# Weight splits of a decoder layer moved within the attention steps, blocks of normed rows rebuilt from their parts, and another split of the last norm

## The chip, the cores and the metric

The kernel runs on one core of one Trainium2 chip. The metric is the device time of one execution in microseconds (us). Inputs are float32, and the kernel keeps float32 accuracy by splitting each matmul operand into a high and a low part (type float32r) and adding three products: high by high, high by low, low by high.

## What is computed

One decoder layer on 512 rows of width 1024. The input is normed, and one projection gives the inputs of two branches: sparse attention (an indexer picks 128 of 512 keys for each query; 8 heads share a latent of rank 128) and a gated short convolution. Each branch is projected, multiplied by a sigmoid gate, and the sum goes through one output projection and a norm. A gated MLP with a convolution of width 3 and a per-layer embedding (PLE) with its own gate follow, and a last norm.

```python
h = layer_norm(x, ln_emb_g, ln_emb_b)
proj = h @ w_in[i]
...
o_lat = dsa_sparse_attention(q_lat, c_kv, q_idx, k_idx, w_idx)
att = jnp.einsum('bshr,hrd->bshd', o_lat, w_uv[i]).reshape(bsz, seq, ATT_WIDTH)
conv_y = cv_b * causal_dwconv(cv_c * cv_x, mix_conv_w[i], mix_conv_b[i])
merged = (jax.nn.sigmoid(g_att + b_gate[i, 0]) * (att @ w_br_att[i])
          + jax.nn.sigmoid(g_conv + b_gate[i, 1]) * (conv_y @ w_br_conv[i]))
h = layer_norm(DEEPNORM_ALPHA * h + merged @ w_o[i], ln1_g[i], ln1_b[i])
gu = causal_dwconv(h @ w_ffn_up[i], ffn_conv_w[i], ffn_conv_b[i])
g_ffn, u_ffn = jnp.split(gu, 2, axis=-1)
ffn = (jax.nn.silu(g_ffn) * u_ffn) @ w_ffn_down[i]
ple = jax.nn.sigmoid(h @ w_ple_gate[i] + b_ple_gate[i]) * (p[i] @ w_ple[i])
h = layer_norm(DEEPNORM_ALPHA * h + ffn + ple, ln2_g[i], ln2_b[i])
```

## The kernel before

The program is a list of steps, each of which is mostly one weight tile (128 x 1024 float32, a `Chunk`) and its 24 matmuls. `run` (L1356) goes through them in order: for step i it first calls `advance(i)`, then the small jobs hung on that step (`preps`), then the step itself. The instructions of each engine run in the order in which they are written down here, so a job's place in this list is its place in the queue of its engine.

`advance(i)` (L1338) does the weights. It splits the tiles that are due, mostly three steps before they are needed: `Chunk.split` (L53) has ScalarE copy the raw tile into the high part (L62), and `low` (L122, L123) subtracts that from the raw tile to give the low part, on VectorE (`lo="v"`) or GpSimd (`lo="p"`). As soon as a raw tile is used up, SyncE loads a later one; four raw tiles, four high and four low ones are in rotation.

From `at_first` on a list called `order` gives the steps: a convolution step (place 0), the four query projections (1 to 4), nine more convolution steps (5 to 13), then gates and branch projections from place 14 to 37. At eleven of them, places 12, 14, 16, 18, 20, 21, 22, 24, 26, 27 and 28 (`ATT_AT`), `with_att` (L786) puts a part of the attention ahead of the step's own matmuls. Such a part (`att_step`, L639) works on three blocks at once: latent output of the block two back (`att_c`: matmuls `ol`, evacuated by ScalarE and VectorE), transposes of the probabilities of the block one back (`att_b`: `pT`, matmuls of L606, which read `p`), and the logits of a new block (`att_a`: matmuls `lg`, their maximum on VectorE at L586 and L589, exponentials on ScalarE at L592, scaling of `p` by VectorE at L598). Tiles at places up to 28 have their low part made by GpSimd, later ones by VectorE. VectorE also works off the search for the top 128 keys (L535, L537) between the steps; it ends about place 13. GpSimd adds the taps of the convolution (L679), which VectorE then reads at L695.

DMAs on GpSimd's queue add up weights in DRAM (`weight_add`, L1056) that the MLP reads later: 28 of them, one at each place from 8 to 35. Copies that they need go out on SyncE's queue at places 0 to 13.

After the output projection (`wo_half1`, one step for each block of 128 rows) comes the first norm (`ln1`, L876): VectorE statistics, GpSimd's power (`rstd`, L155), VectorE's two passes L879 and L880. The block before is then transposed (`ln1_T`, `put_T`, L97): TensorE's transposes L105, an evacuation into high (ScalarE, L126) and low (VectorE, L127) parts, and a third copy of the same PSUM tile by ScalarE (L111) into `hblock`. During the steps of the PLE gate (`ple_gate`, `ple_gate1`, eight steps before the MLP) VectorE forms differences of these blocks (`row_sums`, L1065 and L1067) and splits them (`row_parts`), for the part of the MLP that works by blocks (`by_blocks`), which multiplies them.

The last norm (`last_norm`, L1279) of block 2 is shared: ScalarE and GpSimd do columns 0 to 447 (L1288 to L1290), VectorE the rest (L1295, L1299). Block 3 ends the kernel: its last sums (L1221), statistics, GpSimd's `rstd` and VectorE's four passes, then the stores.

Of the kernel before, what the change touches and what calls it, by code (L numbers as in the profile page):

```python
# [13 lines left out]
P = 128  # L14
# [51 lines left out]
class Kern:  # L66
# [27 lines left out]
        self.hTt = [self.main.tile([P, 4, 2, S], F32R, name=f"{name}{i}", tag="hT", bufs=2) for i in range(2)]  # L94
        self.hT = [self.hTt[c // 4][:, c % 4] for c in range(KC)]

    def put_T(self, b, h, keep=None):  # L97

        nc = self.nc
        tb = slice(b * P, (b + 1) * P)  # L100
        for g in range(2):
            t = self.ps("xT")
            for i in range(4):
                c = 4 * g + i
                nc.tensor.transpose(t[:, i * P:(i + 1) * P], h[:, c * P:(c + 1) * P], self.ident)  # L105
            t4 = t.rearrange("p (c t) -> p c t", c=4)
            self.evac_split(self.hTt[g][:, :, 0, tb], self.hTt[g][:, :, 1, tb], t4)
            if keep is not None:
                if b % 2 == 0:
                    keep[g, b // 2] = self.k4(f"hr{g}{b // 2}", F32, (P, 4, 256))  # L110
                nc.scalar.copy(keep[g, b // 2][:, :, b % 2 * P:b % 2 * P + P], t4)  # L111

    def k2(self, name, dt=F32, shape=(P, 512)):
        return self.main.tile(list(shape), dt, name=name, tag="k2", bufs=8)
# [337 lines left out]
    def plan(self):  # L452
        nc, a = self.nc, self.a
        self.steps = []
        self.chunks = []
        self.preps = {}
        self.nd = self.ns = 0

        def chunk(src, **kw):
            c = Chunk(self, src, **kw)  # L460
            self.chunks.append(c)
            return c
# [9 lines left out]
        def wa(i, **kw):  # L472
            return chunk(a["w_a"][i], **kw)
# [310 lines left out]


        def with_att(n, fn):  # L786
            def f():
                att_step(n)()
                fn()
            return f  # L790

# [12 lines left out]
        order += [("g", j, i) for j in (6, 7) for i in range(2)] + [("r", 3, 1), ("r", 3, 0)]  # L804
        for i, o in enumerate(order):
            if o[0] == "g":
                w = wa(20 + 2 * o[1] + o[2], lo="p" if i <= max(att_at) else "v")
                fn = gate(o[1], o[2], w)
            elif o[0] == "r":
                w = chunk(a["w_br"][2 * o[1] + o[2]], lo="p" if i <= max(att_at) else "v")  # L810
                fn = branch(o[1], o[2], w)
            elif o[0] == "q":
                w = wa(4 + o[1], lo="v" if o[1] == 1 else "p")
                fn = qatt(o[1], w)
            else:
# [14 lines left out]


        self.h1 = []
        self.hblock = {}

        def res_load():

# [46 lines left out]
        def ln1_T(b):  # L883
            if b == 0:
                self.new_hT("h1T")
            self.put_T(b, self.h1[b], self.hblock)

        def wo_half1(b, ws):
            def f():
# [161 lines left out]
        def weight_add(j, i):  # L1051
# [3 lines left out]
                        (s1[:, :512], s0[:, 512:]), (s1[:, 512:], u[:, :512]))[i]  # L1055
            return lambda: nc.gpsimd.dma_start(to, what, accum_op=OP.add, max_dma_last_dim=4096)  # L1056

        def row_sums(n):
# [80 lines left out]

        at_ff = len(self.steps)  # L1140
        for n in range(4):
            self.preps.setdefault(at_ff - 7 + n // 2, []).append(row_sums(n))
            self.preps.setdefault(at_ff - 4 + n, []).append(row_parts((0, 2, 1, 3)[n]))
        late_step, when = None, []
        for j in range(NF):
            if j in BY_BLOCKS:
                ws = [wa(36 + 2 * j)] + [chunk(t) for t in wsum[j]]
                for n, w in enumerate(ws):
                    step(by_blocks(j, n, w), [w])
                late_step = j  # L1150
                continue
            for which in (0, 1):
                when.append(len(self.steps))
                w = wa(36 + 2 * j + which)
                step(ffn(j, which, w), [w])
                if late_step is not None:
                    w = wa(37 + 2 * late_step, cols=(512, 1024))
                    step(by_blocks(late_step, 3, w), [w])
                    late_step = None
        self.preps.setdefault(len(self.steps), []).append(do_later)  # L1160
        for n, (j, i) in enumerate((j, i) for i in range(2) for j in BY_BLOCKS):
            self.preps.setdefault(at_first + n, []).append(weight_copy(j, i))
        for n, (j, i) in enumerate((j, i) for i in (0, 3, 1, 2) for j in BY_BLOCKS):
            self.preps.setdefault(at_first + 8 + n, []).append(weight_add(j, i))
        for n, (name, i) in enumerate(copies):
            self.preps.setdefault(at_first + self.SUM_AT + n, []).append(sum_copy(name, i))
            self.preps.setdefault(when[n], []).append(sum_add(name, i))
# [109 lines left out]
            return mv, self.rstd(mv[:, 1:2])  # L1277

        def last_norm(b):  # L1279
            by_pool = (0, 0, 448, 0)[b]  # L1280
            z, st = self.h1[b], self.st2[b]
            rows = self.out[b * P:(b + 1) * P, :]
            gb = [[t[q.start // 512][:, q.start % 512:][:, :q.stop - q.start] for t in (self.g2, self.b2)]
                  for q in (slice(0, by_pool), F1, slice(by_pool, 512))]
            if by_pool:
                mv, r, nmr = self.ln_aggr(st)
                q = slice(0, by_pool)
                nc.scalar.activation(z[:, q], z[:, q], AF.Identity, bias=nmr, scale=r)  # L1288
                nc.gpsimd.tensor_tensor(z[:, q], z[:, q], gb[0][0], op=OP.mult)
                nc.gpsimd.tensor_tensor(z[:, q], z[:, q], gb[0][1], op=OP.add)  # L1290
            else:
                mv, r = self.mv2.pop(b) if b in self.mv2 else mean_rstd(st)
            qs = list(zip([F1, slice(by_pool, 512)], gb[1:]))
            for q, (g, _) in qs:
                nc.vector.scalar_tensor_tensor(z[:, q], z[:, q], mv[:, 0:1], g, op0=OP.subtract, op1=OP.mult)  # L1295

# [58 lines left out]

    def run(self):  # L1356
        for i, fn in enumerate(self.steps):
            self.advance(i)
            for f in self.preps.get(i, ()):
                f()  # L1360
            fn()
# [99 lines left out]
```

## Time and profile before

| | us |
|---|---|
| median of 3 runs | 768.21 |
| lowest, highest | 768.02, 770.25 |
| the profiled execution | 769.37 |
| its span, first to last instruction | 767.3 |
| of it with TensorE busy | 749.9 |
| with VectorE, ScalarE, GpSimd busy | 557.5, 365.6, 247.1 |
| mean granted TensorE clock | 0.992 |

Engines in the rows: PE is TensorE (PEld its weight loads), DVE VectorE, ACT ScalarE, POOL GpSimd, SP SyncE. A row of the timeline gives start, duration, engine, line, operation, tiles written and read, the count of merged instructions, and in brackets the idle time before it and what ended it. TensorE's matmuls overlap, so their starts tell more than their durations: in steady work one of 512 columns starts every 0.227 us.

### The profile page before, as it was taken

The numbers are of one execution on the slowest core, as the hardware profiler recorded it, in microseconds if no ns is written. First come the engines' busy times: TensorE is split into PE (matmuls) and PEld (weight loads), VectorE is DVE, ScalarE is ACT, GpSimd is POOL, SyncE is SP. The second block draws the span as 40 slices with busy tenths as digits, with TensorE's granted clock in tenths as the row PEclk, the third lists the DMA queues.
The fourth block names the chain that finished last, engine by engine and source line by source line (L and its number), as shares of the span: only waits on it lengthen the run. The fifth ranks groups of instructions, "written<-read, shape, count | busy, mean of one in ns | idle before, by whom it ended". The sixth has DMA issues, their size and how long they took to land.

```text
span 767.3 us, 10309 instructions
## 1 busy us (share of the span) xinstructions
PE 749.9 (98%) x3831; PEld 635.5 (83%) x3831; DVE 557.5 (73%) x888; ACT 365.6 (48%) x561; POOL 247.1 (32%) x201
## 2 busy tenths in 40 slices
PE   7999999989999999999999999999999999999995
PEld 5998888878878888888788999998998888888885
DVE  5878999765655457958667777877777656788697
ACT  4556434466566425233335555555553433565540
POOL 4324666753415118956312311011112110100002
PEclk9999999999999999999999999999999999999998
DMA  8362576774323636996536756676668842656561
GB/s 322 103 236 94 167 218 191 207 192 110 99 66 95 140 130 253 299 339 212 220 110 234 190 179 184 178 203 195 189 192 213 199 136 70 205 180 233 187 210 56
DMA packets 41267, 138.84 MB, mean 181 GB/s; under 512 B 4945, under 2 KB 5073, under 8 KB 40833
## 3 DMA queue, kind: packets, MB, share of 16 engines
q1 hardware_dynamic: 31584, 112.21, 41.5%
q0 software_dynamic: 8624, 23.73, 16.5%
q10 hardware_dynamic: 1008, 2.25, 0.8%
q8 instruction: 30, 0.49, 0.2%
q14 instruction: 21, 0.16, 0.1%
HBM read 132.92 MB, written 45.09 MB: 232 GB/s over the span
## 4 chain that ended last, share of the span: by engine, by line
PE 74%; DVE 15%; POOL 3%; issue 3%; DMA 2%; ACT 2%; SPq 0%; DVEq 0%; POOLq 0%; ACTq 0%
PE ffb L1085 9%; PE ff L138 7%; PE ff L137 7%; PE ff L139 7%; PE dn L1215 4%; PE dn L1216 4%; PE dn L1214 4%; PE gt L137 3%; PE gt L138 3%; PE gt L139 3%; DVE tk L537 3%; DVE m L535 3%; DVE score L525 3%; POOL wl L123 2%; PE br L137 2%
## 5 line engine op out<-in xcount | busy, mean ns | idle before, releaser
L123 DVE TENSOR_TENSOR wl<-wr,wh 128x1024 fp32r<-128x1024 f32 x128 | 163.1, 1283 | 54.8 <-ACT wh L62 54.7
L62 ACT CAST wh<-wr 128x1024 fp32r<-128x1024 f32 (+1 forms) x163 | 164.2, 1011 | 80.9 <-PE dn L1216 35.0
L123 POOL TENSOR_TENSOR wl<-wr,wh 128x1024 fp32r<-128x1024 f32 x35 | 88.3, 2524 | 87.3 <-ACT wh L62 82.9
L137 PE MATMUL ff<-h1T,wh 128*128 128x512 f32 x240 | 93.5, 390 | 0.0
L138 PE MATMUL ff<-h1T,wh 128*128 128x512 f32 x240 | 93.5, 390 | 0.0
L139 PE MATMUL ff<-h1T,wl 128*128 128x512 f32 x240 | 93.4, 389 | 0.0
L665 DVE SCALAR_TENSOR_TENSOR ff<-ff,vec,ff 128x511 f32<-128x511 f32 x30 | 22.4, 747 | 47.6 <-ACT ff L664 47.6
L664 ACT ACTIVATE ff<-ff,vec 128x512 f32<-128x512 f32 x30 | 23.4, 779 | 65.5 <-PE ff L139 65.2
L139 PEld LDWEIGHTS ff<-h1T,wl 128*128 128x128 f32 x240 | 45.1, 188 | 9.4
L137 PEld LDWEIGHTS ff<-h1T,wh 128*128 128x128 f32 x240 | 45.1, 188 | 9.0
L138 PEld LDWEIGHTS ff<-h1T,wh 128*128 128x128 f32 x240 | 45.1, 188 | 8.9
L137 PE MATMUL gt<-hT,wh 128*128 128x512 f32 x128 | 51.1, 399 | 0.5 <-DVE ol L127 0.5
L138 PE MATMUL gt<-hT,wh 128*128 128x512 f32 x128 | 50.2, 393 | 0.0
L139 PE MATMUL gt<-hT,wl 128*128 128x512 f32 x128 | 50.1, 391 | 0.0
L155 POOL TENSOR_TENSOR rstd<-veps,neghalf 128x1 f32<-128x1 f32 x12 | 11.6, 963 | 107.9 <-DVE veps L153 81.0
L1016 POOL TENSOR_TENSOR T<-T,B 128x256 f32<-128x256 f32 x11 | 9.2, 835 | 99.0 <-DVE T L1014 99.0
L1020 POOL TENSOR_TENSOR T<-T,ff 128x256 f32<-128x256 f32 x11 | 8.1, 737 | 98.9 <-DVE T L1012 98.9
L1085 PE MATMUL ffb<-hsh,wl 128*128 128x256 f32 x112 | 31.7, 283 | 0.0
L1085 PE MATMUL ffb<-hsl,wh 128*128 128x256 f32 x112 | 31.7, 283 | 0.0
L1085 PE MATMUL ffb<-hsh,wh 128*128 128x256 f32 x112 | 31.7, 283 | 0.0
L137 PE MATMUL cv<-hT,wh 128*128 128x512 f32 x80 | 31.4, 392 | 0.0
L139 PE MATMUL cv<-hT,wl 128*128 128x512 f32 x80 | 31.1, 389 | 0.0
(318 smaller groups left out, 2002.2 us busy)
## 6 DMA issues: line engine op xcount, KB each, us to landing
wr<-in_w_a SPq DMA_DIRECT2D x73, 512.0 KB, 3.7
wr<-in_w_b SPq DMA_DIRECT2D x17, 512.0 KB, 4.6
wr<-in_w_dn SPq DMA_DIRECT2D x15, 512.0 KB, 3.3
ws<-in_w_a SPq DMA_DIRECT2D x28, 256.0 KB, 5.5
wr<-ws SPq DMA_DIRECT2D x14, 512.0 KB, 3.9
wr<-in_w_br SPq DMA_DIRECT2D x8, 512.0 KB, 3.3
ws<-in_w_a POOLq DMA_DIRECT2D x14, 256.0 KB, 5.6
ws<-ws POOLq DMA_DIRECT2D x14, 256.0 KB, 7.3
```

The lines of the kernel that those rows point to most:

```text
L62: nc.scalar.copy(hi, raw)
L123: (self.nc.vector if eng == "v" else self.nc.gpsimd).tensor_tensor(lo, raw, hi.bitcast(F32), op=OP.subtract)
L137: t.matmul(out, wh, xh, start=start, stop=False)
L138: t.matmul(out, wh, xl, start=False, stop=False)
L139: t.matmul(out, wl, xh, start=False, stop=stop)
L525: nc.vector.scalar_tensor_tensor(sc, rl, self.widx[b][:, h:h + 1], prev, op0=OP.mult, op1=OP.add)
L535: nc.vector.max(m8, cur)
L664: nc.scalar.activation(dst, src, AF.Identity, bias=v[:, bcol:bcol + 1], scale=v[:, wcol + 2 * tap:wcol + 2 * tap + 1])
L1085: nc.tensor.matmul(o, l[:, c], r, start=start and c + i == 0, stop=stop and c == 3 and i == 2, skip_group_check=True)
L1214: nc.tensor.matmul(o, ah, wh[:, i, c], start=first, stop=False, skip_group_check=bank == "X")
L1215: nc.tensor.matmul(o, ah, wl[:, i, c], start=False, stop=False, skip_group_check=bank == "X")
L1216: nc.tensor.matmul(o, al, wh[:, i, c], start=False, stop=last, skip_group_check=bank == "X")
```

## The change

Six edits:

1. At the eleven places with an attention part, `advance` moves from ahead of the step to between the attention part and the step's own matmuls. The jobs in `preps` then stand ahead of both.
2. Tiles of places 16 to 28 have their low part made by VectorE, not GpSimd: 13 tiles.
3. The 28 `weight_add` DMAs are put at places 8 to 28, four to every three places, instead of at 8 to 35, one to each.
4. `put_T` no longer makes the third copy. `row_block` has VectorE add the high and the low parts into the blocks, two at the second and two at the third step of the PLE gate; `row_sums` move two steps later.
5. The last norm of block 2: ScalarE and GpSimd take columns 0 to 511, VectorE 512 to 1023.
6. The loop that lays out the MLP's steps is written in another way, with the same order of steps and tiles for the blocks in use (1, 3, 5 to 13 by twos).

```diff
-    def put_T(self, b, h, keep=None):
+    def put_T(self, b, h):
...
-            self.evac_split(self.hTt[g][:, :, 0, tb], self.hTt[g][:, :, 1, tb], t4)
-            if keep is not None:
-                if b % 2 == 0:
-                    keep[g, b // 2] = self.k4(f"hr{g}{b // 2}", F32, (P, 4, 256))
-                nc.scalar.copy(keep[g, b // 2][:, :, b % 2 * P:b % 2 * P + P], t4)
+            self.evac_split(self.hTt[g][:, :, 0, tb], self.hTt[g][:, :, 1, tb],
+                            t.rearrange("p (c t) -> p c t", c=4))
...
+        self.own_advance = set()
...
         def with_att(n, fn):
+            i = len(self.steps)
+            self.own_advance.add(i)
+
             def f():
                 att_step(n)()
+                self.advance(i)
                 fn()
...
-                w = wa(20 + 2 * o[1] + o[2], lo="p" if i <= max(att_at) else "v")
+                w = wa(20 + 2 * o[1] + o[2], lo="p" if i < 16 else "v")
...
-                w = chunk(a["w_br"][2 * o[1] + o[2]], lo="p" if i <= max(att_at) else "v")
+                w = chunk(a["w_br"][2 * o[1] + o[2]], lo="p" if i < 16 else "v")
...
+        def row_block(g, h):
+
+            def f():
+                t = self.hblock[g, h] = self.k4(f"hb{g}{h}", F32, (P, 4, 256))
+                hi, lo = (self.hTt[g][:, :, i, 256 * h:256 * h + 256].bitcast(F32) for i in range(2))
+                nc.vector.tensor_tensor(t, hi, lo, op=OP.add)
+            return f
...
-            self.preps.setdefault(at_ff - 7 + n // 2, []).append(row_sums(n))
+            self.preps.setdefault(at_ff - 7 + n // 2, []).append(row_block(n // 2, n % 2))
+            self.preps.setdefault(at_ff - 5 + n // 2, []).append(row_sums(n))
...
-            self.preps.setdefault(at_first + 8 + n, []).append(weight_add(j, i))
+            self.preps.setdefault(at_first + 8 + 3 * n // 4, []).append(weight_add(j, i))
...
-            by_pool = (0, 0, 448, 0)[b]
+            by_pool = b == NB - 2
...
-                q = slice(0, by_pool)
-                nc.scalar.activation(z[:, q], z[:, q], AF.Identity, bias=nmr, scale=r)
-                nc.gpsimd.tensor_tensor(z[:, q], z[:, q], gb[0][0], op=OP.mult)
-                nc.gpsimd.tensor_tensor(z[:, q], z[:, q], gb[0][1], op=OP.add)
+                nc.scalar.activation(z[:, F0], z[:, F0], AF.Identity, bias=nmr, scale=r)
+                nc.gpsimd.tensor_tensor(z[:, F0], z[:, F0], gb[0][0], op=OP.mult)
+                nc.gpsimd.tensor_tensor(z[:, F0], z[:, F0], gb[0][1], op=OP.add)
...
-            qs = list(zip([F1, slice(by_pool, 512)], gb[1:]))
+            qs = [(F1, gb[1])] + ([] if by_pool else [(F0, gb[0])])
...
         for i, fn in enumerate(self.steps):
-            self.advance(i)
+            if i not in self.own_advance:
+                self.advance(i)
```

## Rows read from the trace of the kernel before

**Rows 1.** The page: busy time, share of the span and instructions of each engine.

```profile
PE 749.9 (98%) x3831; PEld 635.5 (83%) x3831; DVE 557.5 (73%) x888; ACT 365.6 (48%) x561; POOL 247.1 (32%) x201
```

**Rows 2.** Busy time by stretches of 20 us, with granted clock, DMA share, GB/s.

```profile
160.00:180.00 20.00, 17.97 (x85) 14.49 (x84) 11.83 (x24) 15.57 (x27) 9.35 (x6) 0.91 0.61 152
```

**Rows 3.** The waits of PE: for whom, us in total, times, longest.

```profile
PE pT L606 <- DVE p L598: 2.4, 2, 2.0
...
PE xT L105 <- DVE hr L880: 1.5, 1, 1.5
```

**Rows 4.** Timeline of PE about 160 to 168.

```profile
163.67 0.77 PE L606 MATMUL pT<-ident,p 128*128 128x128 f32 x5 [2.03 <-DVE p L598]
...
166.17 0.80 PE L137 MATMUL gt<-hT,wh 128*128 128x512 f32 x1
...
168.40 0.39 PE L139 MATMUL gt<-hT,wl 128*128 128x512 f32 x1
```

**Rows 5.** Timeline of DVE, 151 to 164.

```profile
151.22 0.69 DVE L695 TENSOR_TENSOR cvy<-cv,cvt 128x512 f32<-128x512 f32 x1 [0.98 <-POOL cvt L679]
...
156.12 1.86 DVE L589 TENSOR_SCALAR nmx<-mx 128x4 f32<-128x4 f32 x1
...
160.35 3.27 DVE L598 TENSOR_SCALAR p<-p,rs 128x256 f32<-128x256 f32 x4
```

**Rows 6.** Timeline of POOL, 155 to 158.

```profile
155.32 2.63 POOL L123 TENSOR_TENSOR wl<-wr,wh 128x1024 fp32r<-128x1024 f32 x1
```

**Rows 7.** Timeline of DVE, 169 to 174: L589 and L598 with no GpSimd work beside them.

```profile
169.45 0.17 DVE L589 TENSOR_SCALAR nmx<-mx 128x4 f32<-128x4 f32 x1
...
172.41 1.41 DVE L598 TENSOR_SCALAR p<-p,rs 128x384 f32<-128x384 f32 x4
```

**Rows 8.** Low parts: duration ns min/median/max; GpSimd's at 150 to 248, VectorE's of all.

```profile
L123 POOL TENSOR_TENSOR wl<-wr,wh x13: 2346/2397/2643, 151.1 to 245.1; 128x1024 fp32r<-128x1024 f32 x13
...
L123 DVE TENSOR_TENSOR wl<-wr,wh x128: 678/1219/3429, 24.5 to 748.9; 128x1024 fp32r<-128x1024 f32 x114, 128x512 fp32r<-128x512 f32 x14
```

**Rows 9.** Timeline of DVE, POOL and PE, 215 to 221.

```profile
215.09 3.30 DVE L598 TENSOR_SCALAR p<-p,rs 128x256 f32<-128x256 f32 x4
215.86 2.38 POOL L123 TENSOR_TENSOR wl<-wr,wh 128x1024 fp32r<-128x1024 f32 x1 [6.30 <-ACT wh L62]
...
218.45 0.77 PE L606 MATMUL pT<-ident,p 128*128 128x128 f32 x5 [0.38 <-DVE p L598]
...
220.93 0.47 PE L137 MATMUL gt<-hT,wh 128*128 128x512 f32 x1 [0.47 <-DVE ol L127]
```

**Rows 10.** Timeline of ACT, POOL, DVE and PE, 360 to 370.

```profile
360.22 0.59 ACT L111 COPY hr<-xT 128x512 f32<-128x512 f32 x1 [4.39 <-DVE h1T L127]
...
363.72 2.40 POOL L123 TENSOR_TENSOR wl<-wr,wh 128x1024 fp32r<-128x1024 f32 x1 [5.21 <-ACT wh L62]
363.76 3.44 DVE L879 SCALAR_TENSOR_TENSOR hr<-hr,mv,g 128x1024 f32<-128x1024 f32 x1
...
369.01 1.09 PE L105 MATMUL xT<-ident,hr 128*128 128x128 f32 x8 [1.54 <-DVE hr L880]
```

**Rows 11.** Timeline of DVE and POOL, 757 to 763.

```profile
757.71 1.87 DVE L1299 SCALAR_TENSOR_TENSOR hr<-hr,rstd,b 128x512 f32<-128x512 f32 x2
...
759.57 1.12 POOL L1290 TENSOR_TENSOR hr<-hr,b 128x448 f32<-128x448 f32 x1
...
760.77 1.41 DVE L1295 SCALAR_TENSOR_TENSOR hr<-hr,mv,g 128x512 f32<-128x512 f32 x2
```

**Rows 12.** Busy time of the two stretches in which VectorE gets more work; columns as in rows 2.

```profile
150.00:248.00 98.00, 94.87 (x474) 77.22 (x473) 56.75 (x135) 61.04 (x119) 43.13 (x28) 0.98 0.42 109
...
380.00:420.00 40.00, 40.00 (x182) 33.23 (x181) 25.84 (x28) 17.74 (x25) 5.76 (x5) 1.00 0.45 166
```

**Rows 13.** The page's groups of instructions: mean ns of ScalarE's high parts.

```profile
L62 ACT CAST wh<-wr 128x1024 fp32r<-128x1024 f32 (+1 forms) x163 | 164.2, 1011 | 80.9 <-PE dn L1216 35.0
```

**Rows 14.** The page's DMA issues: KB each, us from issue to landing.

```profile
wr<-in_w_a SPq DMA_DIRECT2D x73, 512.0 KB, 3.7
```

More of the change, by code (lines that the diff above doesn't have):

```diff
@@ L105, in put_T @@
                 nc.tensor.transpose(t[:, i * P:(i + 1) * P], h[:, c * P:(c + 1) * P], self.ident)
-            t4 = t.rearrange("p (c t) -> p c t", c=4)
-            self.evac_split(self.hTt[g][:, :, 0, tb], self.hTt[g][:, :, 1, tb], t4)
-            if keep is not None:
-                if b % 2 == 0:
-                    keep[g, b // 2] = self.k4(f"hr{g}{b // 2}", F32, (P, 4, 256))
-                nc.scalar.copy(keep[g, b // 2][:, :, b % 2 * P:b % 2 * P + P], t4)
+            self.evac_split(self.hTt[g][:, :, 0, tb], self.hTt[g][:, :, 1, tb],
+                            t.rearrange("p (c t) -> p c t", c=4))
     def k2(self, name, dt=F32, shape=(P, 512)):
@@ L832, in plan @@
         self.h1 = []
-        self.hblock = {}
         def res_load():
@@ L885, in ln1_T @@
                 self.new_hT("h1T")
-            self.put_T(b, self.h1[b], self.hblock)
+            self.put_T(b, self.h1[b])
         def wo_half1(b, ws):
@@ L1056, in weight_add @@
             return lambda: nc.gpsimd.dma_start(to, what, accum_op=OP.add, max_dma_last_dim=4096)
+        self.hblock = {}
+        def row_block(g, h):
[4 more added lines that the diff above has]
+            return f
         def row_sums(n):
@@ L1141, in plan, with last_block @@
         for n in range(4):
-            self.preps.setdefault(at_ff - 7 + n // 2, []).append(row_sums(n))
+            self.preps.setdefault(at_ff - 7 + n // 2, []).append(row_block(n // 2, n % 2))
+            self.preps.setdefault(at_ff - 5 + n // 2, []).append(row_sums(n))
             self.preps.setdefault(at_ff - 4 + n, []).append(row_parts((0, 2, 1, 3)[n]))
-        late_step, when = None, []
+        when, left = [], []
+        def last_block():
+            for j in left:
+                w = wa(37 + 2 * j, cols=(512, 1024))
+                step(by_blocks(j, 3, w), [w])
+            left.clear()
         for j in range(NF):
             if j in BY_BLOCKS:
-                ws = [wa(36 + 2 * j)] + [chunk(t) for t in wsum[j]]
-                for n, w in enumerate(ws):
+                for n in range(3):
+                    w = chunk(wsum[j][n - 1]) if n else wa(36 + 2 * j)
                     step(by_blocks(j, n, w), [w])
-                late_step = j
+                    if n == 0:
+                        last_block()
+                left.append(j)
                 continue
@@ L1155, in plan @@
                 step(ffn(j, which, w), [w])
[L1156 to L1159, printed above, removed]
+                last_block()
         self.preps.setdefault(len(self.steps), []).append(do_later)
@@ L1279, in last_norm @@
         def last_norm(b):
-            by_pool = (0, 0, 448, 0)[b]
+            by_pool = b == NB - 2
             z, st = self.h1[b], self.st2[b]
             rows = self.out[b * P:(b + 1) * P, :]
-            gb = [[t[q.start // 512][:, q.start % 512:][:, :q.stop - q.start] for t in (self.g2, self.b2)]
-                  for q in (slice(0, by_pool), F1, slice(by_pool, 512))]
+            gb = [[t[h] for t in (self.g2, self.b2)] for h in range(2)]
             if by_pool:
                 mv, r, nmr = self.ln_aggr(st)
-                q = slice(0, by_pool)
-                nc.scalar.activation(z[:, q], z[:, q], AF.Identity, bias=nmr, scale=r)
-                nc.gpsimd.tensor_tensor(z[:, q], z[:, q], gb[0][0], op=OP.mult)
-                nc.gpsimd.tensor_tensor(z[:, q], z[:, q], gb[0][1], op=OP.add)
+                nc.scalar.activation(z[:, F0], z[:, F0], AF.Identity, bias=nmr, scale=r)
+                nc.gpsimd.tensor_tensor(z[:, F0], z[:, F0], gb[0][0], op=OP.mult)
+                nc.gpsimd.tensor_tensor(z[:, F0], z[:, F0], gb[0][1], op=OP.add)
             else:
                 mv, r = self.mv2.pop(b) if b in self.mv2 else mean_rstd(st)
-            qs = list(zip([F1, slice(by_pool, 512)], gb[1:]))
+            qs = [(F1, gb[1])] + ([] if by_pool else [(F0, gb[0])])
             for q, (g, _) in qs:
```

## The prediction

> **What bounds the kernel now.** I read the page's busy times first: TensorE is busy nearly all of the span, so a faster helper engine gains nothing by itself [rows 1]. The question is only where TensorE waits, and whether the change reaches that place. The list of its waits answers this: after the start-up two matter, transposes of attention probabilities that wait for VectorE's scaling (2.4 us in two places) and transposes of the first norm's result that wait for VectorE's second pass (1.5 us) [rows 3]. Then the windows, for waits that the idle time does not show: the stretch 160 to 180 alone has a granted clock of 0.91 [rows 2]. The two levels are 1.2 and 2.4 GHz, so 0.09 x 20 / 0.5 = 3.6 us of it ran at the lower one. The timeline puts this behind the idle 2.03 us: between the gate's matmul at 166.17 and the one at 168.40 five starts take 2.23 us, where five steady ones take 5 x 0.227 = 1.14, so 1.09 us more is lost [rows 4]. All that the change can win lies in these few microseconds and in the tail behind the last matmul.
>
> **Edits 1 and 2, first place (160 to 168).** The chain that ends in the stall goes: convolution product L695, ScalarE's split of the next tile, ScalarE's and VectorE's copies of transposes, maximum, its negative (L589), exponentials, scaling (L598), transposes. Two VectorE operations in it are far too long: L589 on four columns takes 1.86 us, and the scaling of four pieces of 256 columns 3.27 us [rows 5]. Beside the first runs GpSimd's low part, 155.32 to 157.95, and L589 ends 0.03 us after it [rows 6]; another lies under the scaling. Undisturbed, L589 takes 0.17, and four pieces of 384 columns take 1.41 [rows 7], so four of 256 take at most that. VectorE thus stands still while GpSimd works, and 13 of GpSimd's low parts, 2.40 us each, go [rows 8]. They return on VectorE at 1.22 us each, 13 x 1.22 = 15.9 us.
> The new end of the chain: 160.35 + 3.27 = 163.62 before. Off: about 1.7 at L589 (1.86 less 0.17), 3.27 - 1.41 = 1.86 at the scaling, 1.01 for ScalarE's high part, which now stands behind the exponentials [rows 13]. On: the low part of place 16, which VectorE must do ahead of L695, where it is idle only because it waits for GpSimd's taps [rows 5]: 1.22. That is 160.3. The waiting transposes could have gone at 163.67 - 2.03 = 161.6 [rows 4], so 1.3 us are to spare and the wait of 2.03 goes; with no such idle I take the slow matmuls to go too: 2.03 + 1.09 = 3.1 us. The bounds: 1.0 (the first rival) and 3.1.
>
> **Second place (217 to 221).** The same picture, smaller: scaling 3.30 us with a GpSimd low part inside it, transposes 0.38 us late, and behind them the gate 0.47 us late, because VectorE's evacuations come after that scaling [rows 9]. With 1.41 at most in place of 3.30 the evacuations can start 1.9 us earlier, less the 1.22 of the low part now put between: still 0.7 earlier. I count both waits: 0.85 us, with 0.4 as the lower bound. What is late next there is the eight PSUM banks filling up, which leaves a few tenths of waits that I do not count as won.
>
> **What the moved step costs elsewhere.** A split comes later by its attention part, but its tile is needed three steps on, at least 3 x 24 x 0.227 = 16.3 us; if that cover went, TensorE would wait at the gate for the difference. Queued behind the moved splits: on ScalarE the next sigmoid, on VectorE the gate's products and the next attention part's evacuations, on SyncE the load of a later raw tile, which takes 3.7 us [rows 14] and has four steps. Past VectorE's queue: 56.75 busy of 98 us, 72.6 with the 15.9 [rows 12]. I put these at 0, up to +1.
>
> **Edit 3.** The same DMAs, issued up to seven places earlier. GpSimd has 43.13 busy us in the stretch [rows 12], of which 13 x 2.40 = 31.2 go; what is left is 12 us with 13 issues and two convolution operations in it, under 0.9 each. Their copies on SyncE's queue go out at places 0 to 13, ahead of each sum; the sums are read in the MLP, beyond 420 us. Cost 0; without the cover an issue ahead of the taps, 0.9.
>
> **Edit 4, first norm.** The stall at 369.01 comes from one GpSimd low part: it starts at 363.72, VectorE's pass L879 starts at 363.76 and takes 3.44 instead of about 1.3, and `rstd`, which L880 needs, stands behind it in GpSimd's own queue [rows 10]. That low part is so late because its high part stands on ScalarE behind the third copies (L111), the first of which waits 4.39 us for VectorE [rows 10]. Without them ScalarE does both evacuations of that block at once and the high part some 5 us sooner, GpSimd's low part follows the `rstd` of block 1, and block 2's norm meets it no more. The wait of 1.54 us goes; lower bound 0, if it meets the next pass instead.
> VectorE gains four additions, like a low part two float32 inputs of 1024 columns, so 4 x 1.22 = 4.9 us, in a stretch with 25.84 busy of 40 [rows 12]: 30.7 of 40. Its weight splits there run more than a step ahead of TensorE; the price if that cover went is what VectorE lags beyond it, so 0 to +1. I take 0.
>
> **Edit 5, tail.** GpSimd's last addition for block 2, 1.12 us for 448 columns, ends at 760.69, and block 3's pass L1295 starts 0.08 us behind it [rows 11]. 64 columns more are 1.12 x 64 / 448 = 0.16 on each of GpSimd's two operations and about 0.1 on ScalarE's, so GpSimd ends 0.4 later and holds VectorE so much longer. VectorE's two small pieces of 64 columns go, one of which waits inside the 1.87 us of L1299 [rows 11]; that brings the last sums some 0.3 sooner, in vain if L1295 is held. Cost +0.35, between -0.3 and +0.6. Edit 6 leaves the order of the work as it is: 0.
>
> **Sum.** -3.1 - 0.85 - 1.54 + 0.35 = -5.1 us. Against the profiled execution, 769.37, that is 764.2; this one lies 1.16 above the median of 768.21, so the median should be 763.1. With every bound at its good end -5.8, 762.4.
>
> **Rivals.**
> *VectorE's own split takes the lock's place at 161.* GpSimd still makes the low part of place 15, now between the attention part and the convolution of place 12, ahead of the taps. If that delays the taps by a whole low part, 2.4 [rows 8], the 1.3 to spare become 1.1 of idle and the clock may fall again, 1.09: of 3.1 about 1.0 is won. Sum -3.0, median 765.2. For it: L695 waits for the taps already [rows 5]. Against it: ScalarE's tap products are late too, and cover most of that low part.
> The Trainium skill, page SBUF — State Buffer, section Who interferes with whom, says that a VectorE instruction with two SBUF inputs and a GpSimd instruction that reads SBUF exclude each other, whoever starts first blocking the other for its whole length. By this rule the new splits on VectorE are themselves such instructions, and the tap adds and the split of place 16 can block one another, which speaks for this rival; L879 under GpSimd's low part [rows 10] agrees with it.
> *The first norm keeps its stall*: block 2's norm meets GpSimd at another moment. Sum -3.6, median 764.6. Against: `rstd` of block 2 then stands ahead of nothing but its own chain.
> *It does not do what it says.* The stalls at 161 and 369 re-form with other releasers, 0.5 won in all: 767.7.
> *Slower: the splits stand in front of the evacuations.* VectorE takes its queue in order. If a low part, waiting for ScalarE's high part, stands ahead of the latent output's evacuation, TensorE fills its eight banks and waits, as at 218 and 220.9, 0.85 us [rows 9], in each of the six attention parts that have transposes and no such stall now: +5.1, with the first two stalls kept, -1.54 and +0.35: +3.9, median 772.1. It decides from the point where a split ends later than the evacuation's input is ready by more than the few tenths that free banks give. For it: VectorE's 15.9 us more. Against: ScalarE's high parts come before the sigmoids, and the scaling gets shorter by more than a split lasts.
>
> **How the numbers follow.** The measurement of this kernel can tell about 0.3%, 2.3 us, from no change. Forecast 0.58, the first rival 0.16, the norm's 0.08, no effect 0.10, slower 0.08. Faster, below 765.9: 0.58 + 0.08 + three quarters of the first rival, 0.12, so 0.78; same 0.04 + 0.10 = 0.14; slower 0.08. The range leaves out the slow rival and some of no effect above, and goes 1.8 below the forecast for the few tenths at the banks and a lighter tail: 761.3 to 767.3.
>
> **What would show it.** Right: GpSimd without low parts from 150 to 250, scaling of 256 columns under 1.5 us, no PE row waiting for L598 near 161, granted clock 1.00 there, transposes of block 2 in the first norm without a wait, the last GpSimd addition ending later against the last matmul. Wrong: a wait of TensorE near 161 for VectorE or for a bank of equal size, a fall of the clock at another place, gates waiting for a low part, or the norm's passes again at 3 us.

## The result and the profile after

The changed kernel takes 762.97 us (median of 5 runs, 762.01 to 765.05). The kernel before, timed on the same chip beside it, takes 770.06 (5 runs, 768.02 to 771.99). The ratio is 0.9921 [0.9902, 0.9941]: faster, by 0.8%. 763.1 was forecast, within 761.3 to 767.3. The profiled execution of after took 764.64, with a span of 762.8 and a mean granted clock of 0.994.

Lines of the kernel after lie 3 to 4 lower in most places: L119 is the low part (L122, L123 before), L595 the scaling of `p` (L598), L603 the transposes of `p` (L606), L142 the logits (L146), L123 VectorE's evacuations (L127), L692 the convolution's product (L695). L879, L880 and L105 keep their numbers.

From the page of after: busy times, which answer [rows 1], and the chain of work that ended last, by engine.

```profile
PE 748.9 (98%) x3831; PEld 635.7 (83%) x3831; DVE 562.0 (74%) x903; ACT 361.7 (47%) x553; POOL 218.1 (29%) x188
...
PE 95%; DVE 3%; DMA 1%; ACT 0%; issue 0%; SPq 0%; DVEq 0%; ACTq 0%
```

GpSimd has lost 29 us; VectorE has gained 4.5, far less than the work put on it, since its long operations beside GpSimd went (the scalings together take 8.8 us less). TensorE is as busy as before. The head of the list of PE's waits, answering [rows 3]:

```profile
PE ckv L312 <- DVE hT L281: 2.2, 1, 2.2
PE warm L295 <- POOL ident masks.py:199: 1.4, 1, 1.4
PE ckv L308 <- ACT hT L277: 1.2, 2, 0.8
...
```

Both waits of [rows 3] are gone: no row of the whole list names the scaling or the norm's second pass. A new one of 2.2 us stands in the start-up, where the change moves no job (more of it in the part on the start-up). Windows of after, columns as in [rows 2]:

```profile
24.00:30.00 6.00, 6.00 (x39) 6.00 (x39) 4.21 (x8) 2.01 (x4) 2.59 (x4) 0.76 0.47 66
...
160.00:180.00 20.00, 20.00 (x106) 16.50 (x106) 13.35 (x30) 17.27 (x33) 8.69 (x11) 1.00 1.09 214
```

TensorE is busy for all of 160 to 180, at a granted clock of 1.00 where it was 0.91; what the mean clock of 0.994 still lacks lies in the start-up (0.76 in 24 to 30) and behind the last matmuls (0.66 in 755 to 762). The timeline of POOL, DVE and PE about the first place, answering [rows 4], [rows 5] and [rows 6] (this execution runs 2.62 us later than before's up to there, because of the start-up):

```profile
148.75 2.40 POOL L119 TENSOR_TENSOR wl<-wr,wh 128x1024 fp32r<-128x1024 f32 x1 [4.43 <-ACT wh L62]
151.12 2.64 POOL L676 TENSOR_TENSOR cvt<-cvt,tap 128x511 f32<-128x511 f32 x2
...
152.73 2.11 DVE L119 TENSOR_TENSOR wl<-wr,wh 128x1024 fp32r<-128x1024 f32 x1
154.76 0.68 DVE L692 TENSOR_TENSOR cvy<-cv,cvt 128x512 f32<-128x512 f32 x1
...
157.42 4.17 POOL L1056 DMA_DIRECT2D ws<-in_w_a  x5
...
158.72 0.28 DVE L586 TENSOR_SCALAR nmx<-mx 128x4 f32<-128x4 f32 x1
...
161.37 1.14 DVE L595 TENSOR_SCALAR p<-p,rs 128x256 f32<-128x256 f32 x4
...
163.78 1.03 PE L603 MATMUL pT<-ident,p 128*128 128x128 f32 x8
164.74 1.34 PE L142 MATMUL lg<-kT,qa 64*128 64x384 f32 x12
166.01 0.50 PE L133 MATMUL gt<-hT,wh 128*128 128x512 f32 x1
```

The negative maximum takes 0.28 us instead of 1.86, the scaling 1.14 instead of 3.27, and it ends at 162.51, 1.27 us ahead of the first of the eight transposes that read it. GpSimd's last low part up to 250 us is the one at 148.75. Beside the negative maximum it issues DMAs now (157.42), and they do not hold VectorE as the low part did. The second place (DVE, PE; [rows 9]) and the first norm (ACT, POOL, DVE, PE; [rows 10]) of after:

```profile
213.98 1.14 DVE L595 TENSOR_SCALAR p<-p,rs 128x256 f32<-128x256 f32 x4
215.04 1.22 DVE L119 TENSOR_TENSOR wl<-wr,wh 128x1024 fp32r<-128x1024 f32 x1
...
217.44 1.32 PE L142 MATMUL lg<-kT,qa 64*128 64x384 f32 x12
```

```profile
354.06 1.07 ACT L62 CAST wh<-wr 128x1024 fp32r<-128x1024 f32 x1
...
356.33 3.38 POOL L119 TENSOR_TENSOR wl<-wr,wh 128x1024 fp32r<-128x1024 f32 x1
...
360.86 1.27 DVE L879 SCALAR_TENSOR_TENSOR hr<-hr,mv,g 128x1024 f32<-128x1024 f32 x1
362.58 1.31 DVE L880 SCALAR_TENSOR_TENSOR hr<-hr,rstd,b 128x1024 f32<-128x1024 f32 x1 [0.44 <-POOL rstd L151]
...
365.17 1.03 PE L105 MATMUL xT<-ident,hr 128*128 128x128 f32 x8
```

ScalarE's high part is made at 354.06 instead of 362.59, GpSimd's low part is over 1.15 us before the norm of block 2 begins, and the transposes have no wait.

To see where the time went, I took the start of every matmul in after less the start of the same one before. The difference changes in few places, and these are the terms of the sum:

| place | forecast | after | changed kernel, second profile |
|---|---|---|---|
| start-up, to 25 us | 0 | +2.6 | 0.0 |
| 161 to 178 | -3.1 | -3.74 | -3.74 |
| 217 to 226 | -0.85 | -1.04 | -1.05 |
| 366 to 376, first norm | -1.54 | -1.77 | -1.77 |
| last matmul to VectorE's last pass | +0.35 | +0.07 | +0.47 |

The second profile is that of an execution of the changed kernel (762.4 us) whose start-up runs as before's does. Elsewhere the difference moves by less than 0.1 at a step.

### The profile page after: what moved, and what is told of

Read it like the earlier page. It is cut to its first block, busy times and chain, and to the rows that moved or that the text cites. A ratio compares the mean times of both kernels' runs of the same rounds, so it can differ in the third digit from the quotient of the medians.

```text
span 762.8 us, 10310 instructions
## 1 busy us (share of the span) xinstructions
PE 748.9 (98%) x3831; PEld 635.7 (83%) x3831; DVE 562.0 (74%) x903; ACT 361.7 (47%) x553; POOL 218.1 (29%) x188
## 4 chain that ended last, share of the span: by engine, by line
PE 95%; DVE 3%; DMA 1%; ACT 0%; issue 0%; SPq 0%; DVEq 0%; ACTq 0%
PE ffb L1095 9%; PE ff L133 7%; PE ff L135 7%; PE ff L134 7%; PE dn L1232 5%; PE dn L1233 5%; PE dn L1231 5%; PE gt L133 4%; PE gt L134 4%; PE gt L135 4%; PE cv L133 2%; PE cv L135 2%; PE cv L134 2%; PE br L133 2%; PE wo L754 2%; PE pg L753 2%
## 5 line engine op out<-in xcount | busy, mean ns | idle before, releaser
L119 DVE TENSOR_TENSOR wl<-wr,wh 128x1024 fp32r<-128x1024 f32 x141 | 177.5, 1269 | 45.3 <-ACT wh L62 45.3
L119 POOL TENSOR_TENSOR wl<-wr,wh 128x1024 fp32r<-128x1024 f32 x22 | 56.8, 2583 | 34.9 <-ACT wh L62 24.8
L744 POOL TENSOR_TENSOR mT<-sig,mT 128x512 fp32r<-128x512 f32 x8 | 13.1, 1664 | 85.4 <-ACT mT L743 85.4
```

What stands on the lines that cost most here:

```text
L119: (self.nc.vector if eng == "v" else self.nc.gpsimd).tensor_tensor(lo, raw, hi.bitcast(F32), op=OP.subtract)
```

## Experiments

My theory was that of the prediction: VectorE stands still beside GpSimd's low parts, and the late scaling costs the first two places, the late norm the third. The rivals: that only the order of ScalarE's and VectorE's queues counts (edit 1 alone), that the number of low parts on GpSimd counts (edit 2 alone), and that splits on VectorE stand in front of evacuations.

### Edit 2 alone: low parts on VectorE, still ahead of the attention part

```diff
-                w = wa(20 + 2 * o[1] + o[2], lo="p" if i <= max(att_at) else "v")
+                w = wa(20 + 2 * o[1] + o[2], lo="p" if i < 16 else "v")
-                w = chunk(a["w_br"][2 * o[1] + o[2]], lo="p" if i <= max(att_at) else "v")
+                w = chunk(a["w_br"][2 * o[1] + o[2]], lo="p" if i < 16 else "v")
```

> The kernel before with edit 2 alone: low parts of places 16 to 28 by VectorE, the advance where it was. Theory (GpSimd's low parts block VectorE, and the order matters as well): L589 near 161 falls from 1.86 to under 0.4 us and the scaling of 256 columns from 3.27 to 1.1 to 1.4, but the split of place 17 now stands ahead of the attention part in VectorE's queue, 1.22 us, and ScalarE's high part, 1.0, is still ahead of its copies: the transposes near 161 still wait, 0.3 to 1.2 us, with or without a fall of the clock. The second place (217 to 221) gains 0.8 to 1.0. From 25 us on 2 to 3.5 us are won. Rival (the engine is all that counts): the wait near 161 is gone, 3.7 us won there, as in the changed kernel. Rival (the order is all that counts): the wait stays at 1.5 us or more.

Measured: 767.02 us (766.42 to 770.66), ratio 0.9978 [0.9957, 0.9999]. The matmuls win 3.21 us at the first place, and no wait near 161 is listed any more. Both edits together win 3.74 there, so a part is left to edit 1, but as slower matmuls and not as the wait that I had expected: the scaling ends at 161.48, when the transposes, from 161.02, have begun, and from their start to the gate's there are 2.78 us, where after has 2.23. The second place wins 1.05. But 2.29 us are given back between, 1.84 of them at 181. Timeline of this kernel, ACT, DVE and PE:

```profile
160.34 1.14 DVE L598 TENSOR_SCALAR p<-p,rs 128x256 f32<-128x256 f32 x4
...
177.37 1.05 ACT L62 CAST wh<-wr 128x1024 fp32r<-128x1024 f32 x1
...
178.45 1.23 DVE L123 TENSOR_TENSOR wl<-wr,wh 128x1024 fp32r<-128x1024 f32 x1 [1.51 <-ACT wh L62]
179.59 0.42 DVE L127 TENSOR_TENSOR ol<-ol,ol 128x256 fp32r<-128x256 f32 x1
...
181.02 0.47 PE L137 MATMUL br<-cvT,wh 128*128 128x512 f32 x1 [1.79 <-DVE ol L127]
```

VectorE waits 1.51 us for ScalarE's high part, then makes the low part, and only then evacuates `ol`, for which TensorE waits 1.79. This is the mechanism of the prediction's slower rival, at one of the attention parts instead of six.

### Edit 1 alone: advance between the attention part and the step

```diff
+            i = len(self.steps)
+            self.own_advance.add(i)
+
             def f():
                 att_step(n)()
+                self.advance(i)
                 fn()
...
         for i, fn in enumerate(self.steps):
-            self.advance(i)
+            if i not in self.own_advance:
+                self.advance(i)
```

> The kernel before with edit 1 alone: advance between attention part and gate, the low parts still by GpSimd. Theory: ScalarE's high part and so GpSimd's low part come behind the exponentials; L589 is free (0.2 to 0.3 us), and the scaling starts before GpSimd's low part does, at most its last piece is caught. The wait near 161 falls to 0 to 0.5 us, the slow matmuls behind it go: 2.5 to 3.7 us won there, 0.3 to 1.0 at the second place. Rival (the engine is all that counts): scaling still over 2.5 us and the wait near 161 still over 1.5 us.

Measured: 768.4 us (768.24 to 771.08), ratio 0.9992 [0.9974, 1.001]. The first place wins all of its 3.74 us here too, though its scaling still takes 3.3 us: it starts early enough. The second place wins nothing, 1.96 are given back at 195 to 199, and 0.75 at 251. DVE, POOL and PE of this kernel:

```profile
187.28 5.98 DVE L599 TENSOR_SCALAR p<-p,rs 128x512 f32<-128x512 f32 x4
...
188.05 4.92 POOL L123 TENSOR_TENSOR wl<-wr,wh 128x1024 fp32r<-128x1024 f32 x2 [10.63 <-ACT wh L62]
...
193.31 1.64 PE L607 MATMUL pT<-ident,p 128*128 128x128 f32 x13 [1.01 <-DVE p L599]
```

Two of GpSimd's low parts, 4.92 us, now fall together upon another scaling, which takes 5.98 us. The stall has moved, not gone.

### Edits 1 and 2

> The kernel before with edits 1 and 2 together, nothing else. Theory: the same course as the changed kernel up to the first norm: from 25 us to the second place 4.8 us won (3.8 near 161, 1.0 near 220), and the stall of 1.5 us at the first norm is still there. Rival (the earlier additions of weights, edit 3, have a part in it): less than 4.3 or more than 5.3 won by 300 us.

The two diffs above together. Measured: 763.66 us (763.51 to 766.75), ratio 0.9937 [0.9916, 0.9958]. The matmuls win 3.74 us at the first place and 1.02 at the second, and give nothing back; the first norm keeps its wait of 1.54 us. By shifts of matmul starts from 25 us to the end: edit 1 alone -1.0, edit 2 alone -1.9, both -4.7. Each edit alone meets a wait that the other takes away.

### Edit 4 alone: blocks summed from their parts

```diff
-            if keep is not None:
-                if b % 2 == 0:
-                    keep[g, b // 2] = self.k4(f"hr{g}{b // 2}", F32, (P, 4, 256))
-                nc.scalar.copy(keep[g, b // 2][:, :, b % 2 * P:b % 2 * P + P], t4)
...
+                nc.vector.tensor_tensor(t, hi, lo, op=OP.add)
```

> The kernel before with edit 4 alone: no third copy of the transposed rows, blocks added up by VectorE in the PLE gate's steps. Theory: nothing changes before the first norm; there the wait of TensorE for L880, 1.54 us, goes, 1.6 to 1.8 us are won at that place, and VectorE's additions cost nothing behind it: no wait of TensorE from 370 to 440. Rival (GpSimd's low part only meets the next pass): the wait stays, at 0.5 us or more, at block 2 or 3.

Measured: 766.99 us (765.73 to 769.96), ratio 0.9964 [0.9943, 0.9985]. The matmuls win 1.77 us at the first norm, but 0.25 is lost just ahead of it, most of that at 354.6, where the transposes of the block before start later; the whole change shows no such loss. Nothing moves anywhere else, and the four additions of VectorE bring no wait up to 440. The window 160 to 180 keeps its granted clock of 0.91.

### The first norm in another way: the fourth PLE gate tile's low part on VectorE

```diff
-        ws = [wb(10 + kk, resident=True, lo="p") for kk in range(4)]
+        ws = [wb(10 + kk, resident=True, lo="pppv"[kk]) for kk in range(4)]
```

> The kernel before with one low part moved: the last weight tile of the PLE gate's first half (the one at 363.72) by VectorE, the third copies kept. Theory (GpSimd's low part in front of the norm's power is the cause of the wait at 369, not the copies as such): the wait falls from 1.54 to under 0.3 us, though ScalarE's high part still stands behind the copies; L879 takes 1.3 us. Rival (the copies on ScalarE are the cause): the wait stays at 1.2 us or more.

The kernel before, with the third copies left in ScalarE's queue. Measured: 772.24 us (767.94 to 774.52), ratio 1.0017 [0.9994, 1.0041]. The wait at 369 became longer, not shorter. ACT, DVE and PE (this execution is 2.5 us late from the start-up on):

```profile
365.20 1.05 ACT L62 CAST wh<-wr 128x1024 fp32r<-128x1024 f32 x1
...
366.28 1.22 DVE L123 TENSOR_TENSOR wl<-wr,wh 128x1024 fp32r<-128x1024 f32 x1 [1.66 <-ACT wh L62]
367.43 0.68 DVE L895 TENSOR_TENSOR hr<-wo,hr 128x512 f32<-128x512 f32 x1
...
369.25 1.27 DVE L879 SCALAR_TENSOR_TENSOR hr<-hr,mv,g 128x1024 f32<-128x1024 f32 x1
...
372.33 1.09 PE L105 MATMUL xT<-ident,hr 128*128 128x128 f32 x8 [2.23 <-DVE hr L880]
```

L879 takes 1.27 us instead of 3.44, so GpSimd was what lengthened it. But VectorE now waits 1.66 us for the same late high part, makes the low part, and begins the norm's sums 3.0 us later. The late high part is the root, and edit 4 removes it; moving the low part alone exchanges a lock for a queue. That is nearer to the rival of the expectation, the copies on ScalarE, than to its theory.

### Edit 3 alone: earlier sums of weights

```diff
-            self.preps.setdefault(at_first + 8 + n, []).append(weight_add(j, i))
+            self.preps.setdefault(at_first + 8 + 3 * n // 4, []).append(weight_add(j, i))
```

> The kernel before with edit 3 alone: additions of weights at places 8 to 28 instead of 8 to 35. Theory: cost 0, the waits of TensorE stay as they are to 0.3 us, from 25 us on nothing moves by more than 0.5 us. Rival (more issues ahead of GpSimd's own work lengthen the stall near 161): its wait grows to 2.5 us or more.

Measured: 768.01 us (767.18 to 771.38), ratio 0.9978 [0.9956, 1.0]. Its profile has the late start-up (see below); from 45 us to the last matmul its starts lie 2.5 to 2.6 us behind before's, and that moves by less than 0.1. Its fastest five executions (767.2 to 767.4) are some 0.5 under before's fastest (767.7 to 768.1); the trace, which is of a slower execution, does not show where, and this stays open. Behind VectorE's last pass it has 3.18 us to the end of the span, where before's has 3.76: the nine profiles of kernels with edit 2 or edit 3 have 3.2 us there, the five of kernels with neither 3.6 to 3.9. This would fit the half microsecond; its cause is not shown.

### Edit 5 undone: the changed kernel with the old split of the last norm

```diff
-            by_pool = b == NB - 2
+            by_pool = (0, 0, 448, 0)[b]
...
```

> The changed kernel with edit 5 undone: GpSimd and ScalarE take columns 0 to 447 of block 2's last norm, VectorE the rest. Theory: from the last matmul to VectorE's last pass of block 3 the time is that of the kernel before, 3.15 us, where the changed kernel has 3.22; the medians differ by less than 0.3 us. Rival (what was predicted): 0.35 us faster than the changed kernel.

 

> The changed kernel once more, beside the kernels below on one chip. Theory (the start has two courses, told by whether GpSimd's first low part gets ahead of VectorE's low part of the rows near 19 us): its times fall in two groups some 2.6 us apart, about 762.0 and 764.6, and the profile shows the transposes of block 3 of the input (the second row at L260 after 20 us) at 24.6 or at 27.2 us, nothing between. Rival (ordinary scatter): times spread evenly over 762 to 765.

Run beside the changed kernel on one chip: 761.98 us (761.74 to 764.96) with the old split, 762.23 (761.76 to 764.85) with the new. DVE and POOL of the changed kernel's second profile, answering [rows 11]:

```profile
753.60 1.26 POOL L1305 TENSOR_TENSOR hr<-hr,b 128x512 f32<-128x512 f32 x1
...
753.99 2.09 DVE L1310 SCALAR_TENSOR_TENSOR hr<-hr,mv,g 128x512 f32<-128x512 f32 x2
```

The first pass starts inside GpSimd's addition and takes 2.09 us, where 1.41 is its length without. From the last matmul to the start of the last pass there are 3.62 us here, 3.22 in the first profile of after, 3.75 and 3.56 in the two mends below, 3.15 before, and 3.15 with the old split. So there is a cost of 0.1 to 0.6, though one kernel with the old split, the last below, has 3.58 too. From the last pass's end to the end of the span the profiles differ by as much without relation to the split (3.2 us here, in after and with the old split, 3.8 before), and the medians do not tell the two splits apart.

### The start-up

The changed kernel's times fall into two groups, 762.0 to 763.0 and 764.6 to 765.1 in the first set, and what parts them seems to be the order of VectorE's and GpSimd's work at the first weight tile. DVE, POOL and PE of before:

```profile
12.68 1.51 DVE L253 TENSOR_SCALAR x<-x,mv,rstd 128x1024 f32<-128x1024 f32 x1
...
18.60 2.35 DVE L285 TENSOR_TENSOR hT<-hx,hT 128x1024 fp32r<-128x1024 f32 x2
...
20.08 3.15 POOL L123 TENSOR_TENSOR wl<-wr,wh 128x1024 fp32r<-128x1024 f32 x1 [2.23 <-ACT wh L62]
```

The same of after, in its profile:

```profile
12.58 0.81 DVE L249 TENSOR_SCALAR x<-x,mv,rstd 128x1024 f32<-128x1024 f32 x1
...
18.27 4.53 DVE L281 TENSOR_TENSOR hT<-hx,hT 128x1024 fp32r<-128x1024 f32 x2
...
19.28 2.43 POOL L119 TENSOR_TENSOR wl<-wr,wh 128x1024 fp32r<-128x1024 f32 x1 [1.49 <-ACT wh L62]
...
22.85 0.69 PE L312 MATMUL ckv<-wx,hT 128*128 128x200 f32 x4 [2.19 <-DVE hT L281]
```

At 12.6 us VectorE's norm either comes just ahead of GpSimd's next operation (0.81 us) or is held by it (1.51). Where it is not held, GpSimd's low part comes 0.8 us sooner, gets in ahead of VectorE's second `hT`, and TensorE is 2.6 us late from there on. In all four profiles with this course (after, edits 1 and 2, edit 3, and the low part on VectorE at the first norm) the transposes at 20 us start 0.8 to 1.0 us earlier than in before, and those at 24.65 2.5 to 2.6 later; the norm takes 0.81 us in each of them. In nine of the ten others it takes 1.51 to 1.55, and the tenth, the last below, has no low part on GpSimd there. That the times' groups are these courses rests on the executions profiled, 764.6 us with it and 762.4 without, and on the second mend. Two mends of the changed kernel: the first tile's split put behind the statistics of input block 3, and the split put behind that block's norm with its low part on VectorE. The diff is that of the second; in the first the line stands behind `aggr(3)`, and the low part stays on GpSimd.

```diff
-        self.advance(0, 1)
...
+        self.advance(0, 1)
...
-        early = [(wa(8 + i, lo="pv"[i], resident=True), kind) for i, kind in enumerate("cx")]
+        early = [(wa(8 + i, lo="vv"[i], resident=True), kind) for i, kind in enumerate("cx")]
```

> The changed kernel, with the split of the first weight tile written down behind the statistics of input block 3 instead of ahead of them, so that GpSimd's low part stands behind its power for that block. Theory: GpSimd's low part can't get ahead of VectorE's low part of the rows any more, the transposes of block 3 start at 23.5 to 24.8 us in every run, and the slow group of times goes: median 760.5 to 762.2. Point to watch: VectorE's norm of block 3 and GpSimd's low part become free within 0.1 us of each other; if GpSimd wins there, the transposes come at 26 us or later and nothing is won. Rival (the two groups come from somewhere else, the loads for one): two groups 2.6 us apart as before.

The first mend: 763.52 us (763.28 to 765.49), ratio to before 0.9929 [0.9906, 0.9951]. A miss: in the profiled execution the two now meet at the next place. POOL, DVE and PE:

```profile
23.08 2.36 POOL L119 TENSOR_TENSOR wl<-wr,wh 128x1024 fp32r<-128x1024 f32 x1
...
23.15 2.84 DVE L249 TENSOR_SCALAR x<-x,mv,rstd 128x1024 f32<-128x1024 f32 x1 [0.67 <-POOL rstd L151]
...
26.04 1.63 PE L260 MATMUL xT<-ident,x 128*128 128x128 f32 x8 [1.90 <-DVE x L249]
```

GpSimd starts 0.07 us ahead, and a norm of the same size as the one that took 0.81 at 12.58 in after takes 2.84. This execution is the slowest of the six; four lie at 763.3 to 763.5, and no profile shows their course.

> The changed kernel, with the split of the first weight tile behind the norm of input block 3 and its low part made by VectorE. Theory: no GpSimd work on two tensors is left from 18 to 30 us, transposes of block 3 at 23.5 to 24.4 us in every run, one group of times. VectorE has 1.22 us more in front of its work on the second half of the rows; if that is on the path, up to 1.2 us of the gain is given back by 40 us. Median 760.2 to 762.5. Rival (ordinary scatter): two groups as before.

The second mend: 761.8 us, all six runs within 761.5 to 762.1, ratio 0.99 [0.9877, 0.9923]. The later group is gone: of 17 executions of the changed kernel with either split of the last norm 6 lie in it, of these six and the next six none.

> The changed kernel with the first weight tile's low part by VectorE behind the norm of input block 3, and with the old split of block 2's last norm. Theory: one group of times, 761.2 to 761.9, median 761.5, 0.3 to 1 us under the changed kernel's median and without its slow group; last matmul to last pass 3.1 to 3.2 us. Rival (the ends trade against something in between): no faster than 762.0.

The second mend with the old split of the last norm: 761.66 us (761.38 to 762.08), ratio 0.9884 [0.9863, 0.9905], the lowest median here; against the second mend alone its 0.14 us is not to be told from none.

> The kernel before with the first weight tile's low part by VectorE behind the norm of input block 3, nothing else. Theory (the kernel before owes its slowest times, 771.5 to 772.4, to GpSimd's low part at the start): no time above 770.5; median 767.2 to 769.3. The stalls at 161, 218 and 369 are untouched. Rival: times near 772 as before.

The second mend in the kernel before: 768.84 us (767.38 to 769.37), ratio 0.9979 [0.9961, 0.9998]. Of the 29 executions of the kernel before beside it, 12 lie at 771.8 to 772.7; none of these ten does. In its profile the norm at 12.8 takes 0.81 us, as in the late course, but the transposes at 24.65 start 0.6 us sooner than in before, not 2.6 later: without GpSimd's low part that order does no harm. Two groups remain, 767.4 (three runs, mean clock 0.997) and 768.7 to 769.4 (seven, 0.992 to 0.994).

## Why the prediction was right, and where its numbers were off

**First place.** The cause was right, and nearly so the new end of the chain: with 2.62 taken off, the scaling ends at 159.9, for 160.3 forecast (0.9 instead of 1.22 is lost ahead of L692, and the scaling takes 1.14 instead of 1.41). That 1.3 us to spare were forecast and 1.27 are there is chance: the forecast counts to the fourth transpose, the 1.27 to the first. The size was 3.1 and is 3.7. The term that was mis-sized is that of the slow matmuls: I compared the starts from the gate's first matmul on, which came out nearly right (0.97 of the 1.09 counted), and left out the logits ahead of it, in before:

```profile
164.37 1.87 PE L146 MATMUL lg<-kT,qa 64*128 64x384 f32 x12
```

From there to the gate's start at 166.17 are 1.80 us, in after 1.27. The logits ran in part at the lower clock too (0.83 in 164.30 to 165.20, 0.50 in 165.20 to 166.10) and win 0.53, and 0.2 more lies in the transposes, which ran at full clock (1.00 in 163.60 to 164.30). The prediction's own 3.6 us at half clock left room for up to 1.8 us lost, where 1.09 was counted. The whole stretch from the end of the idle time should have been compared with steady work.

**Edits 1 and 2 as one.** The prediction costed them as one sum and put the moved step at 0 elsewhere. This held for the two together. It did not say what each does: at the first place either one takes the wait away (edit 2 alone all but 0.5 us of the gain), the second place is won by edit 2, and elsewhere each alone loses time (1.96 and 0.75 us with GpSimd's low parts kept, 2.29 with VectorE's ahead of the evacuations). What edit 1 buys is the absence of the slower rival: a low part that waits for ScalarE stands behind the evacuations of its place, not in front.

**First rival.** What it was named for happened in part: VectorE's own split was held. Its condition did not: GpSimd's low part of place 15 does not delay the taps, which start at 151.12 in after, 148.50 with the start-up taken off, and at 148.47 in before. The low part of place 16 started beside GpSimd's taps and took 2.11 us instead of 1.22, and the product L692 came 0.9 us later than before when the start-up is taken off (154.76 - 2.62 - 151.22). The spare time took it. The Trainium skill, page SBUF — State Buffer, section Who interferes with whom, has the second to start blocked until the first is done. This trace agrees: 152.73 + 2.11 ends 1.08 behind the taps' end at 153.76, a little less than a low part of 1.22. The 4.53 us at 18.27 agree too, ending 1.09 behind GpSimd's low part; the 2.84 at 23.15, in the first mend, end 0.55 behind it, for a length of 0.81.

**Second place and first norm.** -1.04 and -1.77, where -0.85 and -1.54 were forecast. Both waits went whole, and the few tenths that I did not count as won were won. The edit alone and the low part moved to VectorE show that the norm's stall came from the late high part, as the prediction had it.

**Edits 3 and 6, and the tail.** Edit 3 moves no matmul after the start-up, as forecast, and in after none moves by 0.1 from 376 us to the last, where edit 6 would show. The tail costs between 0.07 and 0.6 to the last pass by the profiles, 0.35 forecast, and nothing that times can show.

**From the profile to the median.** The step that failed is the carrying over: one execution lying 1.16 us above the median was taken for an offset that both kernels share. There is none: the median of 768.21 was that of three runs, and the 29 later ones have 769.36, which is where the profiled one lies. Both kernels have executions with and without the late start-up, 2.6 us apart, and the kernel before has three kinds (767.7 to 768.1, 768.5 to 769.6 and 771.8 to 772.7 among the 29). The sum of the places, start-up aside, is -6.5 to -6.6 up to the last matmul, not -5.5; the forecast of 763.1 lies between the two groups of after, 1 us above the lower. From before's profiled execution to the changed kernel's second one, 769.37 to 762.40, it is 7.0 us: 6.55 up to the last matmul, 0.1 behind it (0.5 lost up to the last pass, 0.6 won behind it), and 0.3 outside the span (2.1 us lie there in before, 1.8 in after), for which no trace shows a cause. So the gain was put 1.8 us too small, and the offset of 1.16 that does not exist made up for most of it: that the median is only 0.1 away is in good part chance.

## What to carry to other kernels

When VectorE and GpSimd share work, a small operation in the chain that feeds TensorE can take ten times its length; look for such rows beside a GpSimd row before taking a stall for a lack of speed. Moving a job to another engine and moving it to another place in the queue belong together: here each alone moved the stall and kept 1.0 or 1.9 of the 4.7 us that both win, and a low part given to VectorE must stand behind what TensorE waits for, with its input already there. And run a kernel's profile more than once: an order of two engines decided by a tenth of a microsecond in the start-up moved the end by 2.6 us, half of the gain that was forecast.

## What the runs showed of the hardware that was not expected

The granted clock does not follow from the length of TensorE's idle time alone. Windows of the kernel before behind its idle 2.03 us, then of the kernel with the fourth tile's low part on VectorE about its idle 2.23 us, which ends at 372.33:

```profile
163.00:166.00 3.00, 2.33 (x17) 1.89 (x17) 1.31 (x3) 2.51 (x6) 2.58 (x3) 0.82 0.54 173
166.00:169.00 3.00, 3.00 (x10) 2.33 (x9) 2.94 (x10) 1.96 (x3) 1.76 (x2) 0.62 0.98 203
```

```profile
370.00:374.00 4.00, 1.77 (x13) 1.54 (x13) 2.43 (x3) 1.07 (x2) 1.12 (x2) 1.00 0.90 346
374.00:380.00 6.00, 6.00 (x28) 4.98 (x27) 5.44 (x9) 1.07 (x2) 2.38 (x3) 1.00 0.72 300
```

Behind the shorter idle time part of the work ran at 1.2 GHz, behind the longer one all of it at 2.4 GHz; an idle 1.79 us at 181 (edit 2 alone) cost no clock either (1.00 in 179 to 185), while in the start-up 1.90 us did (0.72 in 24 to 30, first mend). The two groups that remain of the kernel before with the new start-up, 1.3 to 2.0 us apart at mean clocks of 0.997 and 0.992 to 0.994, would fit executions of the same idle time with and without the fall; no profile here is of an execution without it, so that is argued and not shown.
